# Two layer ends of a float32 encoder trunk: other orders on VectorE and ScalarE, sums of squares on VectorE, one chunk of x on a second queue

## The chip, the cores and the metric

One core of one Trainium2 chip runs the whole kernel. The metric is device time in microseconds of one execution; 0.2% of it, about 2.3 us, is what a measurement of this kernel can tell from no change.

## The reference

The input is x, 512 tokens of 1024 features in float32. Two layers follow, each with an attention part and a dense part, and one last RMSNorm:

```python
for l in range(2):
    h = rmsnorm(x, attn_norm[l])
    proj = h @ w_in[l]                       # 1024 -> 3072: q, k, v of two kinds of heads
    sb_out = stick_breaking_attention(...)   # 8 heads of 64
    df_out = rmsnorm(differential_attention(rope(q), rope(k), v, lam)) * (1 - lambda_init)
    x = x + concat(sb_out, df_out) @ w_o[l]
    h = rmsnorm(x, mlp_norm[l])
    u = square(relu(h @ w_ff1[l]))           # 1024 -> 4096
    x = x + u @ w_ff2[l]                     # 4096 -> 1024
return rmsnorm(x, final_norm)
```

## The kernel before

**Layout.** x lies transposed in SBUF: 8 chunks of 128 features (partitions) by 512 tokens. The host hands over the weights cut into pieces of 128 x 1024.

**Products.** Each float32 operand is split into a rounded part (`hi`, written by ScalarE with a copy, L116 for weights, L228 for activations) and a residue (`lo`, written by VectorE with a subtraction, L117 and L229). A product is three matmuls: hi*hi (L281), hi*lo or lo*hi (L282, L283). So TensorE waits for ScalarE's part in the first and for VectorE's part in another. A scheduler orders each engine's instructions by its own costs; `behind(a, b)` (and `in_order`, which chains it) fixes that `a` stands after `b` on one engine.

**Start.** The 8 chunks of x, and the first two weight pieces in four parts of two chunks each, are loaded by SP's queue in one row (L187, L190); ScalarE's queue loads only the gains (L184). Then chunk by chunk `make_h` (L227) writes `h_hi` and `h_lo`, and `split_part` (L103) splits the weights. DMA completions are kept on eight semaphore lanes, which SP's and ScalarE's loads share in program order, so each load waits for the one eight places ahead of it.

**Middle of a layer.** `wo(0)` (L691) adds the second half of the output projection to x, one chunk (`db`) after another: VectorE adds the PSUM bank to x (L704), `make_h` writes the chunk of the next h, `add_sq` (L233) squares it on ScalarE (L237) and adds the square to `ssq` on GpSimd (L238). In the dense part `rms_a` (L244) transposes and reduces `ssq` on TensorE and VectorE, takes the power -1/2 on GpSimd and writes diagonals; `rms_b` spreads the result. It runs beside the first matmuls of the dense part, since the row scale is applied after the product (L824).

**End of a layer.** w_ff2 is applied by a Strassen-like scheme: seven products (`FORMS`: 11, x3, x2, 22, x1, 21, x4), each 256 x 512 in two banks, which `gather` (L849) adds into SBUF tiles `y`. Tiles are then combined: `merge` (L858) is an accumulating DMA, `join` (L855) a VectorE add over 128 x 1024. After product x1 the join of x1 into x3 and that of x1 into 22 follow; product 21 and product x4 remain. `place(tb, j)` says where a finished block lies: tokens tb (128 each), feature half j; half 1 of tokens 0 and 1 lies in x3, of tokens 2 and 3 in 22; half 0 in x4 and 21. In layer 0, `back(c)` (L873) transposes finished blocks on TensorE and adds them to x; its four first calls stand between the matmuls of products 21 and x4. In layer 1 the last norm is worked out on the finished blocks: `square` (ScalarE, with a sum per row), `root` (a VectorE sum L887 and GpSimd power L889), `weigh` (VectorE times the final gain, L894), and `store`: either ScalarE scales a weighed block (L900) or VectorE scales and weighs at once (L902), then a DMA writes it out (L904), from ScalarE's queue for weighed blocks and from SP's for the others. Two lists, `first` for VectorE and `squares` for ScalarE, hold the order.

Of the kernel before, what the change touches and what calls it, by code (L numbers as in the profile page):

```python
# [85 lines left out]
class _Weights:  # L86
    def __init__(self, nc, dram, rawp, splp):
        self.nc, self.dram, self.rawp = nc, dram, rawp
        self.loaded = self.split = self.used = self.turn = 0
        self.raw, self.tiles, self.home, self.then = {}, {}, {}, {}  # L90
        self.depth = 3
        self.pools = [splp]
        self.owner = {}

    def load(self, n):
        while self.loaded < min(n, len(_RING)):
            i = _RING[self.loaded]
            t = self.rawp.tile([P, 1024], F32, tag="raw", name=f"raw{i}")
            self.nc.sync.dma_start(t, self.dram[self.loaded])
            self.raw[i] = t  # L100
            self.loaded += 1

    def split_part(self, i, a, b):  # L103
        nc = self.nc
        if i not in self.tiles and i in self.home:
            self.tiles[i] = self.home[i]
        if i not in self.tiles:
            k = self.spot(i)
            self.owner[k] = i
            self.turn = k + 1  # L110
            hi = self.pools[k // 2].tile([P, 1024], F32R, tag="whi", name=f"whi{i}")
            lo = self.pools[k // 2].tile([P, 1024], F32R, tag="wlo", name=f"wlo{i}")
            self.tiles[i] = (hi, lo)
        hi, lo = self.tiles[i]
        raw = self.raw[i]
        h = nc.scalar.activation(hi[:, a:b], raw[:, a:b], AF.Copy)  # L116
        self.last = h, nc.vector.tensor_tensor(  # L117
            out=lo[:, a:b], in0=raw[:, a:b], in1=hi[:, a:b].bitcast(F32), op=ALU.subtract)

# [32 lines left out]
def trunk(ctx, tc, xT, w, w2, gains, gfin, lamv, cos, sin, out):  # L152
    nc = tc.nc
# [29 lines left out]
    g_all = cp.tile([P, 42], F32, tag="g", name="g_all")  # L183
    nc.scalar.dma_start(g_all, gains)  # L184
    raws = [wraw.tile([P, 1024], F32, tag="raw", name=f"raw{i}") for i in range(2)]
    for c in range(KC):
        nc.sync.dma_start(x[:, c, :], xT[c])  # L187
        if c % 2 == 0:
            for i in range(2):
                nc.sync.dma_start(raws[i][:, c * P : (c + 2) * P], w[i][:, c * P : (c + 2) * P])  # L190
# [126 lines left out]
    for l in range(L):  # L317
        with ExitStack() as actx:
# [27 lines left out]
            if l == 0:  # L346
                for c in range(KC):
                    if c % 2 == 0:
                        for i in range(2):
                            W.split_part(i, c * P, (c + 2) * P)  # L350
                    opened = make_h(c, gcol("attn", 0, c))
                W.split = 2
            else:
                pts, opened = opened_by.pop()
# [336 lines left out]
            def wo(half):  # L691
                for j in range(4):
                    u = W.next("o")
                    for dd in range(2):
                        db = 2 * j + dd
                        pt = bank("mm" if half else "any", f"wo{l}{half}{db}")
                        for e in range(4):
                            a = u[0][:, e * 256 + dd * P : e * 256 + dd * P + P]
                            b_ = u[1][:, e * 256 + dd * P : e * 256 + dd * P + P]
                            mh, ml = (md_hi, md_lo) if half else (ms_hi, ms_lo)  # L700
                            three(pt, (a, b_), (mh[:, e, :], ml[:, e, :]), e == 0, e == 3)
                            if e < 3:
                                yield 3 * 0.216
                        nc.vector.tensor_add(x[:, db, :], x[:, db, :], pt)  # L704
                        if half == 0:
                            make_h(db, gcol("mlp", l, db))
                            add_sq(db, db == 0, tt)
                        yield 3 * 0.216

            def dense(pts):  # L710
# [58 lines left out]
        with ExitStack() as fctx:  # L769
# [82 lines left out]
                return done  # L852

            def join(to, by):
                nc.vector.tensor_add(y[to], y[to], y[by])  # L855

            def merge(to, by):
                nc.gpsimd.dma_start(  # L858
# [37 lines left out]
            def store(tb, j, weighed):  # L896
                o = place(tb, j)
                r = fin[:, 4 * tb + 7 : 4 * tb + 8]
                if weighed:
                    done = nc.scalar.activation(o, o, AF.Copy, scale=r)  # L900
                else:
                    done = nc.vector.scalar_tensor_tensor(  # L902
                        out=o, in0=o, scalar=r, in1=(cos_t, sin_t)[j], op0=ALU.mult, op1=ALU.mult)
                (nc.scalar if weighed else nc.sync).dma_start(out[tb, :, 512 * j : 512 * j + 512], o)  # L904
                return done

            def in_order(*steps):
# [18 lines left out]
            for g in range(GROUPS):  # L926
# [28 lines left out]
                for f, form in enumerate(FORMS):  # L955
# [6 lines left out]
                    for n, (c, i, r) in enumerate(work):  # L962
                        if c not in held:
                            held[c] = W.next("f")
                        u = held[c]
                        _, hi, lo = forms[2 * c + i]
                        rs = slice(r * P, r * P + P)
                        mine = [m for m, e in enumerate(work) if e[2] == r]
                        three(to[r], (hi[:, SIDE[form], rs], lo[:, SIDE[form], rs]), wpair(u, i, 512),
                              n == mine[0], n == mine[-1])  # L970
                        if tail and last and n == 3:
                            first = [gather("x4", to, (0,))]
                            squares = [square(tb, 0) for tb in (2, 3, 0)]
                            first += [weigh(2, 1), root(2), root(3), weigh(3, 1), root(0)]
                            squares.append(store(2, 1, True))
                        if end and not last and (form, n) in (("21", 5), ("21", 7), ("x4", 1), ("x4", 3)):
                            h = back({"21": 4, "x4": 6}[form] + (n % 4 == 3))
                    if tail:
# [12 lines left out]
                    elif form == "22":  # L991
                        join("22", "x2")
                    elif form == "x1":
                        join("x3", "x1")
                        join("22", "x1")
                        if last:
                            for tb in (0, 1, 2, 3):
                                square(tb, 1)
                            for tb in (0, 1):
                                weigh(tb, 1)  # L1000
            if last:
                first += [gather("x4", to, (1,)), store(0, 0, False), None, store(2, 0, False)]
                squares += [square(1, 0), store(3, 1, True), store(0, 1, True)]
                first[-2] = root(1)
                in_order(*first, store(1, 0, False), store(3, 0, False))
                in_order(*squares, store(1, 1, True))
            else:
                W.pools.pop()
# [76 lines left out]
```

## Time and profile before

| | |
|---|---|
| median of 3 runs | 1161.31 us (1161.12 to 1162.6) |
| profiled execution | 1163.8 us, of it span 1162.0 us |
| granted TensorE clock | 0.998 |
| TensorE matmuls | 1146.6 us busy, 99% of the span |
| VectorE, ScalarE, GpSimd busy | 852.9, 606.2, 191.8 us |
| DMA | 171.67 MB, mean 148 GB/s |

The span is the profiled execution from its first to its last instruction or transfer. "Busy" of TensorE includes overlap of pipelined matmuls, so stalls are read from the starts of consecutive matmuls, which follow each other every 0.227 us where nothing waits. In a timeline row the first number is the start in us, the second the length; an "x2" merges neighbours; the bracket tells how long the engine was idle and who ended it. DVE is VectorE, ACT ScalarE, POOL GpSimd, SPq and ACTq the DMA-issuing side of two engines.

### The profile page before, as it was taken

What the parts mean: (1) busy time and instruction counts of PE and PEld (TensorE: products, weight loads), DVE (VectorE), ACT (ScalarE), POOL (GpSimd) and SP (SyncE); (2) the same over time, 40 slices, a digit from 0 to 9 for tenths busy, and PEclk for the clock granted to TensorE, in tenths of its full rate; (3) what the DMA queues carried; (4) which work ended last, traced back from release to release, by engine and by line L of the source; (5) the groups of instructions that cost most, each with busy time, mean ns of one, the idle gap of its engine ahead of it and who ended that gap; (6) DMA issues with size and microseconds to landing.
All of it is one profiled execution on the core that took longest, in us unless ns stands there. A gap on an engine that the chain in (4) does not pass through costs nothing.

```text
span 1162.0 us, 15297 instructions
## 1 busy us (share of the span) xinstructions
PE 1146.6 (99%) x5458; PEld 951.7 (82%) x5458; DVE 852.9 (73%) x1385; ACT 606.2 (52%) x1075; POOL 191.8 (17%) x271
## 2 busy tenths in 40 slices
PE   9999999999999999999999999999999999999996
PEld 6888888878888888888778888888888888888885
DVE  7888788777556757767888878877676577676676
ACT  6456666545645445445344566665465354453554
POOL 1011543131101001002000125332310010010021
PEclk9999999999999999999999999999999999999999
DMA  7546433146764755737526553432757557467185
GB/s 245 157 145 188 128 109 120 63 177 178 193 178 94 202 158 106 213 134 128 144 73 180 145 165 118 136 91 74 241 121 192 170 92 207 154 99 237 52 155 146
DMA packets 57291, 171.67 MB, mean 148 GB/s; under 512 B 7168, under 2 KB 8192, under 8 KB 57216
## 3 DMA queue, kind: packets, MB, share of 16 engines
q1 hardware_dynamic: 45840, 130.83, 33.9%
q0 software_dynamic: 10656, 38.80, 19.2%
q8 instruction: 43, 0.70, 0.3%
q10 hardware_dynamic: 720, 1.07, 0.2%
q14 instruction: 32, 0.26, 0.1%
HBM read 138.17 MB, written 2.10 MB: 121 GB/s over the span
## 4 chain that ended last, share of the span: by engine, by line
PE 83%; issue 5%; DMA 5%; DVE 4%; ACT 2%; POOL 1%; POOLq 0%; SPq 0%; DVEq 0%; ACTq 0%
PE f L282 9%; PE f L283 9%; PE f L281 9%; PE x L281 4%; PE x L283 4%; PE x L282 4%; PE wo L281 2%; PE wo L282 2%; DMA q<-in_w 2%; PE wo L283 2%; DMA yx<-yx 2%; DVE wlo L117 1%; PE T1s L567 1%; PE T0s L567 1%; DVE h_lo L229 1%
## 5 line engine op out<-in xcount | busy, mean ns | idle before, releaser
L282 PE MATMUL f<-h_lo,whi 128*128 128x512 f32 x512 | 199.3, 389 | 1.0 <-DVE h_lo L229 1.0
L281 PE MATMUL f<-h_hi,whi 128*128 128x512 f32 x512 | 199.7, 390 | 0.0
L116 ACT ACTIVATE whi<-raw 128x1024 fp32r<-128x1024 f32 (+1 forms) x130 | 131.9, 1019 | 129.7 <-PE f L282 40.1
L283 PE MATMUL f<-h_hi,wlo 128*128 128x512 f32 x512 | 199.3, 389 | 0.0
L116 ACT ACTIVATE whi<-q 128x512 fp32r<-128x512 f32 x224 | 128.5, 624 | 120.6 <-PE x L283 45.8
L117 DVE TENSOR_TENSOR wlo<-raw,whi 128x1024 fp32r<-128x1024 f32 (+1 forms) x130 | 153.7, 1187 | 45.1 <-ACT whi L116 44.4
L117 DVE TENSOR_TENSOR wlo<-q,whi 128x512 fp32r<-128x512 f32 x224 | 146.0, 686 | 49.2 <-ACT whi L116 49.0
L282 PEld LDWEIGHTS f<-h_lo,whi 128*128 128x128 f32 x512 | 96.1, 188 | 21.3 <-DVE h_lo L229 1.4
L283 PEld LDWEIGHTS f<-h_hi,wlo 128*128 128x128 f32 x512 | 96.1, 188 | 20.1
L281 PEld LDWEIGHTS f<-h_hi,whi 128*128 128x128 f32 x512 | 96.1, 188 | 19.7
L225 DVE TENSOR_TENSOR Al<-F,Ah 128x256 fp32r<-128x256 f32 (+2 forms) x96 | 74.4, 778 | 44.1 <-ACT Ah L224 44.1
L797 POOL DMA_DIRECT2D q<-in_w x48 | 41.9, 874 | 388.1 <-DVE wlo L117 368.2
L282 PE MATMUL x<-wlo,Ah 128*128 128x512 f32 x256 | 99.7, 390 | 0.7 <-DVE wlo L117 0.7
L281 PE MATMUL x<-whi,Ah 128*128 128x512 f32 x256 | 99.9, 390 | 0.0
L283 PE MATMUL x<-whi,Al 128*128 128x512 f32 x256 | 99.6, 389 | 0.0
L224 ACT ACTIVATE Ah<-F 128x256 fp32r<-128x256 f32 (+2 forms) x96 | 67.2, 703 | 50.4 <-DVE F L833 48.5
L824 DVE SCALAR_TENSOR_TENSOR F<-f,rbc 128x512 f32<-128x512 f32 x64 | 43.5, 687 | 64.9 <-PE f L283 57.6
L825 ACT ACTIVATE F<-F 128x512 f32<-128x512 f32 x64 | 39.7, 624 | 37.2 <-DVE F L824 37.1
L282 PEld LDWEIGHTS x<-wlo,Ah 128*128 128x128 f32 x256 | 48.1, 188 | 11.0 <-DVE wlo L117 1.1
L283 PEld LDWEIGHTS x<-whi,Al 128*128 128x128 f32 x256 | 48.0, 188 | 10.1
L281 PEld LDWEIGHTS x<-whi,Ah 128*128 128x128 f32 x256 | 48.1, 188 | 9.8
L228 ACT ACTIVATE h_hi<-x,g_all 128x512 fp32r<-128x512 f32 x32 | 22.4, 718 | 28.7 <-DVE x L704 17.5
(1055 smaller groups left out, 2556.8 us busy)
## 6 DMA issues: line engine op xcount, KB each, us to landing
raw<-in_w SPq DMA_DIRECT2D x126, 512.0 KB, 4.1
q<-in_w SPq DMA_DIRECT2D x64, 512.0 KB, 4.3
q<-in_w POOLq DMA_DIRECT2D x64, 512.0 KB, 5.4
yx<-yx POOLq DMA_DIRECT2D x6, 512.0 KB, 6.7
x<-in_xT SPq DMA_DIRECT2D x8, 256.0 KB, 4.5
raw<-in_w SPq DMA_DIRECT2D x8, 128.0 KB, 4.4
yx<-y POOLq DMA_DIRECT2D x2, 512.0 KB, 5.7
y<-y POOLq DMA_DIRECT2D x2, 512.0 KB, 8.7
```

What stands on the lines that cost most here:

```text
L116: h = nc.scalar.activation(hi[:, a:b], raw[:, a:b], AF.Copy)
L117: self.last = h, nc.vector.tensor_tensor(out=lo[:, a:b], in0=raw[:, a:b], in1=hi[:, a:b].bitcast(F32), op=ALU.subtract)
L224: nc.scalar.activation(hi, src, AF.Copy)
L225: nc.vector.tensor_tensor(out=lo, in0=src, in1=hi.bitcast(F32), op=ALU.subtract)
L228: a = nc.scalar.activation(h_hi[:, c, :], x[:, c, :], AF.Copy, scale=g)
L281: nc.tensor.matmul(pt, ah, bh, start=first, stop=False)
L282: nc.tensor.matmul(pt, ah, bl, start=False, stop=False)
L283: nc.tensor.matmul(pt, al, bh, start=False, stop=last)
L567: nc.tensor.transpose(pt[:, off : off + P], u["w"][qi][:, kb * P : (kb + 1) * P], ident)
L797: nc.gpsimd.dma_start(t, quad(g, q, c), accum_op=ALU.add)
L824: nc.vector.scalar_tensor_tensor(out=t, in0=pt, scalar=0.0, in1=rbc, op0=ALU.max, op1=ALU.mult)
L825: nc.scalar.activation(t, t, AF.Square)
```

## The change

Five edits, all at the start of layer 0 and at the ends of both layers' parts:

1. Chunk 1 of x is loaded from ScalarE's queue, behind the gains; SP's row has one load less.
2. For the first quarter of the first two weight pieces the rounding, too, is done by VectorE (`eager`).
3. `add_sq` in the middle of both layers adds on VectorE instead of GpSimd (7 adds a layer).
4. After product x1 the join into 22 stands ahead of that into x3, by `in_order`.
5. In the last norm both `weigh` of half 1 of tokens 2 and 3 stand ahead of the first gather of x4 on VectorE, `store(2, 0)` stands ahead of the second gather, `store(3, 1)` ahead of `square(1, 0)` on ScalarE, and `store(3, 0)` ahead of `store(1, 0)`; all stores but the last, (1, 1), are issued by SP.

```diff
+    def round(self, o, src):
+        if self.eager:
+            return self.nc.vector.tensor_copy(o, src)
+        return self.nc.scalar.activation(o, src, AF.Copy)
...
-        h = nc.scalar.activation(hi[:, a:b], raw[:, a:b], AF.Copy)
+        h = self.round(hi[:, a:b], raw[:, a:b])
...
+    nc.scalar.dma_start(x[:, 1, :], xT[1])
     for c in range(KC):
-        nc.sync.dma_start(x[:, c, :], xT[c])
+        if c != 1:
+            nc.sync.dma_start(x[:, c, :], xT[c])
...
                         for i in range(2):
+                            W.eager = c == 0
                             W.split_part(i, c * P, (c + 2) * P)
+                        W.eager = False
...
-                            add_sq(db, db == 0, tt)
+                            add_sq(db, db == 0, tt, nc.vector)
...
-                (nc.scalar if weighed else nc.sync).dma_start(out[tb, :, 512 * j : 512 * j + 512], o)
+                (nc.scalar if (tb, j) == (1, 1) else nc.sync).dma_start(out[tb, :, 512 * j : 512 * j + 512], o)
...
-                            first = [gather("x4", to, (0,))]
+                            first = [weigh(2, 1), weigh(3, 1), gather("x4", to, (0,))]
                             squares = [square(tb, 0) for tb in (2, 3, 0)]
-                            first += [weigh(2, 1), root(2), root(3), weigh(3, 1), root(0)]
+                            first += [root(2), root(3), root(0)]
                             squares.append(store(2, 1, True))
+                            first.append(store(2, 0, False))
+                            squares.append(store(3, 1, True))
...
-                        join("x3", "x1")
-                        join("22", "x1")
+                        in_order(join("22", "x1"), join("x3", "x1"))
...
-                first += [gather("x4", to, (1,)), store(0, 0, False), None, store(2, 0, False)]
-                squares += [square(1, 0), store(3, 1, True), store(0, 1, True)]
-                first[-2] = root(1)
-                in_order(*first, store(1, 0, False), store(3, 0, False))
+                first += [gather("x4", to, (1,)), store(0, 0, False)]
+                squares += [square(1, 0), store(0, 1, True)]
+                first.append(root(1))
+                in_order(*first, store(3, 0, False), store(1, 0, False))
```

As built, the change also moves neighbours: at the start the residues of the second quarter (two L117) stand ahead of chunk 2's `h_lo` on VectorE, no longer behind it, and on ScalarE the second and third `h_hi` follow the first at once; at both joins the second half of a w_ff2 weight residue (L117) now stands right behind the join into x3, in layer 1 ahead of three `weigh`s that it followed; the transposes of the first `rms_a` stand one matmul earlier; and a few roundings, squares and residues of the dense parts' first blocks change places on ScalarE and VectorE.

More of the change, by code (lines that the diff above doesn't have):

```diff
@@ L91, in __init__ @@
         self.depth = 3
+        self.eager = False
         self.pools = [splp]
@@ L854, in join @@
             def join(to, by):
-                nc.vector.tensor_add(y[to], y[to], y[by])
+                return nc.vector.tensor_add(y[to], y[to], y[by])
             def merge(to, by):
```

## The prediction

> **What bounds the kernel now.** I read the page first, then TensorE's waits, then timelines around each wait that the change touches.
>
> ```profile
> span 1162.0 us, 15297 instructions
> PE 1146.6 (99%) x5458; PEld 951.7 (82%) x5458; DVE 852.9 (73%) x1385; ACT 606.2 (52%) x1075; POOL 191.8 (17%) x271
> ```
>
> TensorE is busy for 99% of the span, and the change leaves its matmuls as they are. So it can win only what TensorE waits, and the two ends at which it has nothing to do. Its waits, longest first:
>
> ```profile
> PE f L282 <- DVE h_lo L229: 1.0, 1, 1.0
> PE p L281 <- ACT h_hi L228: 0.8, 1, 0.8
> PE S1d L477 <- DMA st1d3q<-hl1d3k: 0.7, 1, 0.7
> PE x L282 <- DVE wlo L117: 0.7, 1, 0.7
> PE yT L876 <- DVE y L855: 0.7, 1, 0.7
> ```
>
> Four of these five lie where the change works: f at the middle of layer 0, p at the start, x at the end of layer 1, yT at the end of layer 0. S1d lies in layer 1's attention, which it leaves alone. Between these places TensorE's starts follow each other without a hole and every load is triggered by work on the engines, so I take time won at one place as kept to the end.
>
> **Middle of layer 0 (adds of squares): 1.18 us won.**
>
> ```profile
> 249.74 1.38 POOL L238 TENSOR_TENSOR ssq<-ssq,sq 128x512 f32<-128x512 f32 x1 [0.84 <-ACT sq L237]
> ...
> 249.90 1.76 DVE L229 SCALAR_TENSOR_TENSOR h_lo<-x,g_all,h_hi 128x512 fp32r<-128x512 f32 x1
> ...
> 250.08 0.39 PE L283 MATMUL f<-h_hi,wlo 128*128 128x512 f32 x1
> 250.31 0.39 PE L281 MATMUL f<-h_hi,whi 128*128 128x512 f32 x1
> 251.72 0.50 PE L282 MATMUL f<-h_lo,whi 128*128 128x512 f32 x1 [1.02 <-DVE h_lo L229]
> ...
> 818.28 0.69 DVE L704 TENSOR_TENSOR x<-x,wo 128x512 f32<-128x512 f32 x1
> 819.76 0.75 DVE L229 SCALAR_TENSOR_TENSOR h_lo<-x,g_all,h_hi 128x512 fp32r<-128x512 f32 x1 [0.79 <-ACT h_hi L228]
> 821.00 0.69 DVE L704 TENSOR_TENSOR x<-x,wo 128x512 f32<-128x512 f32 x1 [0.49 <-PE wo L283]
> 821.91 1.23 DVE L117 TENSOR_TENSOR wlo<-raw,whi 128x1024 fp32r<-128x1024 f32 x1 [0.23 <-ACT whi L116]
> 823.06 0.75 DVE L229 SCALAR_TENSOR_TENSOR h_lo<-x,g_all,h_hi 128x512 fp32r<-128x512 f32 x1
> 823.15 1.79 POOL L238 TENSOR_TENSOR ssq<-ssq,sq 128x512 f32<-128x512 f32 x1 [1.47 <-ACT sq L237]
> 825.78 0.39 PE L282 MATMUL f<-h_lo,whi 128*128 128x512 f32 x1
> ...
> 14.91 0.69 DVE L238 TENSOR_TENSOR ssq<-ssq,sq 128x512 f32<-128x512 f32 x1 [0.29 <-ACT sq L237]
> ```
>
> The seventh `h_lo` of layer 0 runs beside a GpSimd add and takes 1.76 us; the same one in layer 1 started first, takes 0.75, and there GpSimd's add is long (1.79). TensorE lost 251.72 - 250.31 - 0.23 = 1.18 us to this; layer 1 lost nothing.
>
> The add on VectorE costs 0.69 (last row, the same operation in the start). For a pair of chunks VectorE then needs, by the layer 1 rows less 0.09 overlap each: x 0.60, wait for `h_hi` 0.88, `h_lo` 0.66, add 0.60, x 0.60, wlo 1.14, `h_lo` 0.66, add 0.60 = 5.74 us. TensorE's pair is 24 matmuls of 0.227 = 5.44. VectorE falls behind by 0.3 a pair on top of the first add's 0.6: about 1.2 at the last pair, whose x then comes at 819.5 instead of 818.28 and whose last `h_lo` ends 5.2 later, at 824.7. Its matmul is due at 825.78: 1.0 us spare in layer 1, and as much in layer 0, where the matmul is due at 250.53. So the wait goes. Queued behind the adds are the next weight residues, needed a block (5.4 us) later, and the transposes of `ssq`, which stand after the first block. Six adds stand ahead of the last `h_lo`, so 0.17 more for each would use that up; beyond it each further 0.17 costs 1.0 us a layer. Bounds: 0.9 to 1.2.
>
> **End of layer 0 (order of the joins): 0.85 us won.**
>
> ```profile
> 566.53 1.23 DVE L855 TENSOR_TENSOR yx<-yx,yx 128x1024 f32<-128x1024 f32 x1 [1.14 <-DMA yx<-yx]
> 567.67 1.22 DVE L855 TENSOR_TENSOR y<-y,yx 128x1024 f32<-128x1024 f32 x1
> ...
> 567.86 0.41 PE L876 MATMUL yT<-edge,yx 128*128 128x128 f32 x2 [0.28 <-issue]
> 568.95 0.44 PE L876 MATMUL yT<-edge,y 128*128 128x128 f32 x2 [0.68 <-DVE y L855]
> ```
>
> VectorE idles 1.14 us for the accumulating DMA into x3, then does both joins. The join into 22 waits for no DMA and takes 1.22: put first, it fits into that hole but for 0.1. The x3 join stays where it is, and the two x transposes still start at 567.86. The two y transposes follow 0.24 later instead of 1.09: 0.85. What is late next is that DMA, so the 0.4 lost ahead of 567.86 remains. Bounds 0.6 (the hole filled less well) to 1.25 (both waits gone).
>
> **End of layer 1: 0.95 us won.**
>
> ```profile
> 1148.77 0.68 DVE L117 TENSOR_TENSOR wlo<-q,whi 128x512 fp32r<-128x512 f32 x1
> 1149.37 0.68 DVE L849 TENSOR_TENSOR y<-y,21130_10400 128x512 f32<-128x512 f32 x1
> ...
> 1153.02 0.69 DVE L849 TENSOR_TENSOR yx<-yx,x 128x512 f32<-128x512 f32 x1 [0.20 <-PE x L283]
> ...
> 1149.51 0.50 PE L282 MATMUL x<-wlo,Ah 128*128 128x512 f32 x1 [0.71 <-DVE wlo L117]
> ...
> 1152.06 2.12 POOL L889 TENSOR_TENSOR fin<-fin,mhalf 128x1 f32<-128x1 f32 x3 [10.18 <-DVE fin L887]
> ...
> 1153.16 0.72 ACT L900 ACTIVATE y<-y,fin 128x512 f32<-128x512 f32 x1 [1.07 <-POOL fin L889]
> ...
> 1157.81 0.33 SPq L904 DMA_DIRECT2D out_xT<-y  x1
> ...
> GB/s 0 0 0 0 0 0 225 440 379 266 0 82 430 379 389 287 440 369 430 379 440 369 420 399 410 400 420 399 389 430 389 430 379 440 277 0 0 0 0 0
> ```
>
> The last row is the DMA rate from 1153.5 to 1161.5 in slices of 0.2: after one hole (at 1155.5) the eight stores of 0.256 MB stream at about 390 GB/s, 0.67 us each, until 1160.5. So the end is the first store's time plus eight transfers plus holes, not the last block's arithmetic.
>
> TensorE: the residue that x waits for (1148.77) stood behind both joins and two `weigh`s. As in layer 0, the join into 22 now fills VectorE's wait for the DMA, and the `weigh`s follow the residue: it comes a join (1.14) and two steps of 0.60 sooner, and the waiting of 0.7 goes. But VectorE's row, not TensorE, sets the rest. Ahead of the gathers of 21 (1149.37) it has one join less and one `weigh` more, so they come 0.55 earlier (1.14 - 0.60); the second `weigh` then stands ahead of the first gather of x4, which stays where it was. With the gathers of 21 come the squares and roots of tokens 2 and 3 and the first power; ScalarE's first store moves from 1153.16 to about 1152.6. The stores of (2,0) and (3,1) are ready at 1153.4 and 1153.9 instead of after the second gather, so the hole of 0.35 closes: 0.55 + 0.35 = 0.9, and 0.05 for ScalarE, which no longer issues three stores in its row. The added wait: the second gather of x4 is queued behind `store(2, 0)`, which waits for GpSimd's power, and comes at 1153.3 instead of 1153.02 though its matmuls end 0.9 sooner. The last blocks (1,0) and (1,1) are then issued at about 1156.9, when the stream has work until 1158.2; that is their cover, 0.5 us after the transfer's start-up. SP issues seven stores of 0.33 each and is never the last. Bounds: 0.35 (the power comes no earlier, only the hole closes) to 1.4.
>
> **Start: 0.3 us won, the least certain.**
>
> ```profile
> 2.12 4.73 DMA x<-in_xT
> ...
> 2.00:4.00 2.00, 2.00 (x6) 0.71 (x5) 0.21 (x2) 0.88 (x3) 0.29 (x4) 1.00 0.97 265
> 4.00:5.00 1.00, 1.00 (x6) 0.37 (x4) 0.46 (x1) 0.81 (x2) 0.00 (x0) 1.00 0.67 70
> ...
> 5.08 0.42 ACT L116 ACTIVATE whi<-raw 128x256 fp32r<-128x256 f32 x1 [0.27 <-DMA raw<-in_w]
> ...
> 6.87 1.34 ACT L228 ACTIVATE h_hi<-x,g_all 128x512 fp32r<-128x512 f32 x2 [1.38 <-DMA x<-in_xT]
> 8.11 0.71 ACT L116 ACTIVATE whi<-raw 128x256 fp32r<-128x256 f32 x2
> ...
> 8.96 0.75 DVE L117 TENSOR_TENSOR wlo<-raw,whi 128x256 fp32r<-128x256 f32 x2
> ...
> 9.70 0.39 PE L282 MATMUL p<-h_lo,whi 128*128 128x512 f32 x1
> ```
>
> Chunk 1 is issued at 2.12 and lands at 6.85; `h_hi` of chunks 1 and 2 follow. From the second queue it goes out behind the gains alone, not behind three loads. Meanwhile the second weight piece, landed at 5.08, bounds from below: on VectorE a rounding (0.2 to 0.4, the wlo row's half at most), `h_lo`, wlo, `h_lo` of chunk 1 = 2.2, so 7.3, and the 14th matmul (9.70 before, `h_lo` of chunk 2) at 8.7: 1.0 won at most. From the other side: `h_lo` of chunk 2 now stands behind two residues. If chunk 2 lands no sooner (its `h_hi` starting at 7.54), `h_hi` 0.70, two roundings 0.71, the second residue 0.50 and `h_lo` 0.75 put that matmul at 10.2: 0.5 lost. If it lands in chunk 1's old place, 6.87: 0.1 won. In the fifth microsecond (the two rows that begin with a stretch; their last three columns are clock, DMA share and GB/s) the DMA share is 0.67 at 70 GB/s, room for part of chunk 1 earlier, so I take 0.3. On VectorE the two added roundings lie in its idle time ahead of chunk 1; without that they would cost 0.2 to 0.4 each.
>
> The Trainium skill (DMA: Bandwidth & Descriptors, "Rules for kernel authors") says that spreading DMAs over several issuing engines gives no bandwidth, since all use the same 16 engines, and saves issue time alone. By that rule the gain would be at most one issue slot of SP, 0.45, and the sum 3.4; no run so far shows two such queues under load at the start.
>
> **Sum.** 1.18 + 0.85 + 0.95 + 0.3 = 3.3 us. The profiled execution took 1163.8 (span 1162.0 and 1.8 around it), so 1160.5 with a profile; the median without is 1161.31, so 1158.0.
>
> **Rivals.**
> - The two queues share the DMA engines, and chunk 1 pushes the first weight pieces back; start -0.5. Total 2.5, 1158.8. For it: the share is 0.97 already from 2 to 4. Against it: 0.67 right after. Chance 0.12.
> - The end of layer 1 stays bound by VectorE and the power: only 0.35 there. Total 2.7, 1158.6. Chance 0.10.
> - One middle or end edit does not do what it says (VectorE is late for another reason and TensorE waits as before) beside one of these: total 1.3 to 2.0, about 1159.6. Chance 0.15.
> - Slower: the adds make VectorE the bound of both middles. TensorE begins to wait when an add takes a step of 0.77 (0.60 + 0.17), and the whole is slower from 1.04 on. At GpSimd's 1.38 each of six adds costs 0.78 more, 4.7, less the 1.0 spare 3.7 in each layer; layer 0 had 1.18 of it before. With 2.1 won at the other places: 1161.31 + 3.7 + 2.5 - 2.1 = 1165.4. Against it: the row of 0.69. Chance 0.05.
> - My forecast, 1158.0: 0.58.
>
> The range reaches from all upper bounds together (1.2 + 1.25 + 1.4 + 1.0 = 4.85, 1156.5) to a gain of 1.0 (1160.3), which takes in all but the slower case. Faster by over 0.2% (2.3 us): 0.77, from the forecast and nearly all of the first two rivals; same 0.17; slower 0.06.
>
> **What would show it.** In the changed profile: f <- `h_lo` and yT <- y gone from TensorE's waits, or yT down to 0.1; every `h_lo` near 0.75; x <- wlo gone; the first store near 0.55 earlier against the last matmuls' old place and no zero in the DMA row; 14th matmul of p before 9.7. Wrong: a new wait on `h_lo` in either middle, a new wait at the transposes of `ssq`, or `h_hi` waiting for x beyond 6.9.

## The result

The changed kernel took 1158.43 us (median of 10 runs, 1157.34 to 1161.88) against 1161.78 for the kernel before beside it (10 runs, 1160.39 to 1163.42). The ratio is 0.9976, 95% interval 0.9967 to 0.9984: 2.8 us won, between 1.9 and 3.8. A second comparison, under after_again below, gave 0.9968 (0.9959 to 0.9978), 3.7 us. The forecast was 1158.0, from 1161.31, and 3.3 won.

The profiled execution took 1157.94 us. Its page begins:

```profile
span 1155.8 us, 15280 instructions
...
PE 1145.5 (99%) x5458; PEld 952.6 (82%) x5458; DVE 856.4 (74%) x1401; ACT 606.6 (52%) x1073; POOL 171.0 (15%) x257
```

TensorE's waits in it, all that the view lists (total us, times, longest):

```profile
PE warm L214 <- POOL edge L208: 1.4, 1, 1.4
PE S1d L487 <- DMA st1d3q<-hl1d3k: 0.6, 1, 0.6
PE yT L886 <- issue: 0.4, 1, 0.4
```

The waits for `h_lo`, `wlo`, `y` and `h_hi` are gone. The two profiled spans differ by 6.2 us, nearly twice what the medians differ by (3.35). Where that comes from is the larger part of what follows: the starts of the same matmul in both traces show it to a tenth of a microsecond, and so do the traces of the experiments, each of which has some stages with the code of before and some with the code after.

The middle of layer 0, timeline of the changed kernel (start, us, engine, line, operation, tiles; in brackets the idle time before and its releaser):

```profile
242.05 0.75 DVE L237 SCALAR_TENSOR_TENSOR h_lo<-x,g_all,h_hi 128x512 fp32r<-128x512 f32 x1
...
243.31 0.68 DVE L714 TENSOR_TENSOR x<-x,wo 128x512 f32<-128x512 f32 x1
...
244.78 0.75 DVE L237 SCALAR_TENSOR_TENSOR h_lo<-x,g_all,h_hi 128x512 fp32r<-128x512 f32 x1 [0.79 <-ACT h_hi L236]
...
245.45 0.68 DVE L246 TENSOR_TENSOR ssq<-ssq,sq 128x512 f32<-128x512 f32 x1
...
246.05 0.68 DVE L714 TENSOR_TENSOR x<-x,wo 128x512 f32<-128x512 f32 x1
...
246.65 1.22 DVE L123 TENSOR_TENSOR wlo<-raw,whi 128x1024 fp32r<-128x1024 f32 x1
...
247.79 0.75 DVE L237 SCALAR_TENSOR_TENSOR h_lo<-x,g_all,h_hi 128x512 fp32r<-128x512 f32 x1
...
248.45 0.68 DVE L246 TENSOR_TENSOR ssq<-ssq,sq 128x512 f32<-128x512 f32 x1
...
249.61 0.39 PE L290 MATMUL f<-h_lo,whi 128*128 128x512 f32 x1
```

Every `h_lo` takes 0.75 (the last took 1.76), the adds 0.68, and the matmul that waited 1.02 starts without a wait, 1.07 after its `h_lo` is done (248.54). The forecast's row for a pair of chunks is there: from the sixth `h_lo` to the eighth it takes 5.74, as forecast.

The end of layer 0, timeline:

```profile
563.27 1.22 DVE L865 TENSOR_TENSOR y<-y,yx 128x1024 f32<-128x1024 f32 x1
564.40 1.22 DVE L865 TENSOR_TENSOR yx<-yx,yx 128x1024 f32<-128x1024 f32 x1
...
565.73 0.41 PE L886 MATMUL yT<-edge,yx 128*128 128x128 f32 x2 [0.36 <-issue]
565.97 0.38 PE L886 MATMUL yT<-edge,y 128*128 128x128 f32 x2
```

The two kinds of transposes are 0.24 apart, where they were 1.09. VectorE no longer waits for the accumulating DMA; the joins stand back to back. Counted by the start of the same matmul, this end is 0.84 shorter.

The end of layer 1: the joins, the first gather of 21, the roots, the powers and ScalarE's first two stores:

```profile
1139.43 1.22 DVE L865 TENSOR_TENSOR y<-y,yx 128x1024 f32<-128x1024 f32 x1
1140.57 1.22 DVE L865 TENSOR_TENSOR yx<-yx,yx 128x1024 f32<-128x1024 f32 x1
...
1144.12 0.68 DVE L859 TENSOR_TENSOR y<-y,21130_10400 128x512 f32<-128x512 f32 x1
...
1146.51 0.33 DVE L897 TENSOR_SCALAR fin<-fin 128x1 f32<-128x1 f32 x2
...
1146.81 1.85 POOL L899 TENSOR_TENSOR fin<-fin,mhalf 128x1 f32<-128x1 f32 x3 [9.21 <-DVE fin L897]
...
1147.41 1.34 ACT L910 ACTIVATE y<-y,fin 128x512 f32<-128x512 f32 x2
```

The DMA rate from 1147.5 to 1155.5 in slices of 0.2 us:

```profile
GB/s 0 0 0 0 0 0 0 184 379 430 379 420 399 399 410 410 410 379 440 379 420 389 430 389 430 389 420 379 440 379 440 379 430 154 0 0 0 0 0 0
```

Once it has begun, the stream of stores has no hole. From the start of the last matmul to the end of the span it was 9.42, and is 8.26.

The start, chunks 1 and 2 of `x` as `h_hi` takes them up, and below them the fifth microsecond (last three columns: clock, DMA share, GB/s):

```profile
4.70 0.72 ACT L236 ACTIVATE h_hi<-x,g_all 128x512 fp32r<-128x512 f32 x1 [0.24 <-DMA x<-in_xT]
5.86 0.72 ACT L236 ACTIVATE h_hi<-x,g_all 128x512 fp32r<-128x512 f32 x1 [0.43 <-DMA x<-in_xT]
```

```profile
4.00:5.00 1.00, 1.00 (x4) 0.35 (x3) 0.69 (x2) 0.76 (x2) 0.00 (x0) 1.00 1.03 357
```

Before, chunk 1 was taken up at 6.87 and chunk 2 right behind it; the microsecond that moved 70 GB/s moves 357.

### The profile page after: what moved, and what is told of

The parts are those of the page before. It is cut to its first block, busy times and chain, and to the rows that moved or that the text cites. A ratio compares the mean times of both kernels' runs of the same rounds, so it can differ in the third digit from the quotient of the medians.

```text
span 1155.8 us, 15280 instructions
## 1 busy us (share of the span) xinstructions
PE 1145.5 (99%) x5458; PEld 952.6 (82%) x5458; DVE 856.4 (74%) x1401; ACT 606.6 (52%) x1073; POOL 171.0 (15%) x257
## 4 chain that ended last, share of the span: by engine, by line
PE 93%; DVE 3%; DMA 2%; ACT 1%; issue 1%; POOL 0%; POOLq 0%; ACTq 0%; DVEq 0%
PE f L290 10%; PE f L289 10%; PE f L291 10%; PE x L290 4%; PE x L289 4%; PE x L291 4%; PE wo L289 3%; PE wo L291 3%; PE wo L290 3%; DMA q<-in_w 1%; DVE wlo L123 1%; PE T1s L577 1%; PE T0s L577 1%; PE p L289 1%; PE p L290 1%
```

## Experiments: each part alone

Four kernels are the one before with one part of the change; they share 33 runs of before (median 1163.11).

```diff
# start_alone: chunk 1 on ScalarE's queue, first two roundings on VectorE
+    nc.scalar.dma_start(x[:, 1, :], xT[1])
...
+        h = self.round(hi[:, a:b], raw[:, a:b])
# adds_alone
+                            add_sq(db, db == 0, tt, nc.vector)
# joins_alone, in layer 0 only
+                            in_order(join("22", "x1"), join("x3", "x1"))
# tail_alone: in_order of the joins in layer 1, weighs, gathers, stores, SyncE's queue
```

> Only the two edits of the start: chunk 1 of x on ScalarE's queue, and the first two roundings on VectorE. The two traces so far show the 14th matmul of p at 9.70 before and near 8.86 after, 0.8 to 0.9 sooner, where the prediction had 0.3. Theory (the hole in the fifth microsecond is filled by the second queue, and the rest of the program carries the gain to the end): starts of the same matmul 0.9 sooner from p on to the last block, time 0.9 us less than before. Rival (the prediction's price; the rest was the draw of that one trace): 0.3 us sooner. Second rival: 0.9 is won at p and lost again at a later wait, time 0 to 0.3 less.

> Only the adds of squares in the middles moved to VectorE, in both layers. Theory: layer 0 loses its wait of f for h_lo, 1.18 to 1.3 us sooner from there on, layer 1 stays without a wait, time 1.2 less than before. Rival (VectorE bound in the middle): a new wait of f or wo for h_lo in one layer, gain under 0.5 or a loss.

> Only the order of the two joins at the end of layer 0. Theory: the wait of yT for y of 0.7 and the 1.09 between the two kinds of transposes shrink, 0.85 us sooner from there on, time 0.85 less. Rival (the DMA that accumulates into x3 is late in its turn): 0 to 0.3. In this trace the attention of layer 1, which no edit touches, shows whether its waits (tv1w 0.6, S1d 0.7 before; the first gone after the change) go with the code or with the run.

> Only the edits at the end of layer 1: order of the joins, weighs, gathers and stores, and the stores on SyncE's queue. Theory A (as predicted): 0.95 us less, the wait of x for wlo gone and the stores 0.9 sooner. Theory B (by the pair of traces: the wait gone, 0.99, and 1.16 more behind the last matmul): 2.1 less. They differ in the distance from the last matmul's start to the end of the span: A 9.4 as before, B 8.3.

| part | median us | ratio (95%) | mean span less than before's | mean time outside the span |
|---|---|---|---|---|
| start | 1162.61 | 1.0001 (0.9991 to 1.0011) | 0.52 | 2.14 |
| adds | 1161.56 | 0.9992 (0.9984 to 1.0001) | 1.41 | 1.76 |
| joins | 1163.18 | 1.0002 (0.9993 to 1.0011) | 0.28 | 2.13 |
| tail | 1161.76 | 0.9992 (0.9983 to 1.0001) | 1.82 | 2.15 |

No part alone is told from no change by its time; each interval is 2 us wide. So the times alone decide between few of the theories: of the first ones, only that of joins_alone lies outside its interval, by little (at most 0.8 won), and so does theory B of tail_alone (at most 2.0 won). The spans add up to 4.0 us. Three of the four also have 0.35 us more outside the span than before (1.78), where the whole change has 0.2 to 0.3 more (2.0 to 2.05); nothing recorded lies there, and what it is stays open. With it taken three times the parts give 3.0 us, with the whole change's share taken once 3.8.

The traces say more. **start_alone** has no loss in the middle of layer 0, though its adds are on GpSimd as before, but the same loss in layer 1. Its rows, layer 0 and then layer 1:

```profile
230.80 0.75 DVE L237 SCALAR_TENSOR_TENSOR h_lo<-x,g_all,h_hi 128x512 fp32r<-128x512 f32 x1
...
230.84 1.86 POOL L246 TENSOR_TENSOR ssq<-ssq,sq 128x512 f32<-128x512 f32 x1 [16.81 <-ACT sq L245]
...
805.24 1.87 DVE L237 SCALAR_TENSOR_TENSOR h_lo<-x,g_all,h_hi 128x512 fp32r<-128x512 f32 x1
...
805.27 1.29 POOL L246 TENSOR_TENSOR ssq<-ssq,sq 128x512 f32<-128x512 f32 x1 [16.80 <-ACT sq L245]
```

GpSimd's first add and VectorE's second `h_lo` of the middle start within 0.04 us of each other, and one of them then takes longer than alone: the `h_lo` 1.87 for 0.75, or the add 1.86 for 1.29. Where VectorE loses, it is late and loses again in each later pair, and TensorE waits 1.0 at the end; where GpSimd loses, nobody waits. Over the six traces with plain adds on GpSimd, VectorE lost in 5 of 12 middles: in layer 0 in four of four with the old start and in none of two with chunk 1 on ScalarE's queue, in layer 1 in one of six. So the term of 1.18 is right where it is lost, which in layer 0 was every traced middle behind the old start. Behind the new start, without any other edit, layer 0 lost nothing, so the forecast's terms for start and middle can't simply be added; why the start should matter for what happens at 231 us isn't shown. The Trainium skill (SBUF — State Buffer, "Summary: rules for kernel authors") says that where a VectorE instruction with two SBUF inputs meets a GpSimd one that reads SBUF, the second to issue is blocked until the first is done. The lengths agree (1.86 and 1.87 are nearly 1.29 and 0.75 together). Which of the two loses can't be read from the recorded starts: `h_lo` is recorded first, by 0.03 to 0.04, in all 12 middles and is the one that is late in 5.

**joins_alone** wins little, because the hole that the join of 22 was to fill isn't 1.14 in every run. Its rows, and under them the one row of tail_alone, which has the old order there; then ScalarE's rounding of a weight piece some 6 us ahead of the joins, in before and in joins_alone:

```profile
565.86 1.22 DVE L855 TENSOR_TENSOR y<-y,yx 128x1024 f32<-128x1024 f32 x1
566.99 1.22 DVE L855 TENSOR_TENSOR yx<-yx,yx 128x1024 f32<-128x1024 f32 x1
...
568.31 0.41 PE L876 MATMUL yT<-edge,yx 128*128 128x128 f32 x2 [1.00 <-issue]
568.56 0.38 PE L876 MATMUL yT<-edge,y 128*128 128x128 f32 x2
```

```profile
566.74 1.23 DVE L855 TENSOR_TENSOR yx<-yx,yx 128x1024 f32<-128x1024 f32 x1 [0.57 <-DMA yx<-yx]
```

```profile
559.30 1.15 ACT L116 ACTIVATE whi<-q 128x512 fp32r<-128x512 f32 x2 [2.77 <-DMA q<-in_w]
```

```profile
559.84 2.19 ACT L116 ACTIVATE whi<-q 128x512 fp32r<-128x512 f32 x4 [2.62 <-DMA q<-in_w]
```

In the seven traces with the old order VectorE waited 1.13 to 1.15 for the DMA into x3 in four, 0.84, 0.83 and 0.57 in the others. Where the hole is short, VectorE comes late: that rounding, which waits for its load, starts between 8.20 and 9.21 after the 2600th matmul, and in all fourteen traces VectorE is free for the joins 6.0 to 6.1 behind it, while the DMA lets the x3 join go at 15.4 to 15.9. So what varies here is the landing of a weight load that no edit touches. The join of 22 takes 1.13 in front of x3, so that x3 comes up to 0.56 later than it could, and in joins_alone TensorE waits 1.00 ahead of the x transposes. From the 2600th to the 2690th matmul, seven traces with the old order take 0.25 us more than before's on the mean, six with the new one and the same matmul order 0.42 less: 0.7 won, between 0.3 and 1.1 by the draw.

**tail_alone** has no wait of x for `wlo`, and 8.79 behind the last matmul, halfway between theory A (9.4) and theory B (8.3). Its 1.82 in the span is nearer B (2.1) than A (0.95), but its time, 0.1 lost to 2.0 won, takes in A and not B. What this end is worth is worked out below from the rows.

## Experiments: middle and attention

```diff
# adds_fenced: before, and GpSimd's add waits for h_lo of its chunk
+                            h = make_h(db, gcol("mlp", l, db))
+                            s = add_sq(db, db == 0, tt)
+                            if db:
+                                tc.add_manual_dep(s[1].ins, h[1].ins.name, mybir.DependencyInfo(
+                                    mybir.DependencyClass.Sync, mybir.DependencyReason.DATA), reason="order")
# adds_twice: the changed kernel, a second instruction of the add's size
+                                nc.vector.tensor_tensor(out=ssq, in0=ssq, in1=ssq, op=ALU.max)
```

> The kernel before, with the adds of squares still on GpSimd, but each made to wait until h_lo of its chunk is done, so that the two never run side by side. In four traces with the adds on GpSimd, GpSimd's add and VectorE's second h_lo start 0.03 us apart in each middle; in 4 of 8 middles VectorE's takes 1.87 (and three later ones 1.77), in the other 4 GpSimd's takes 1.86. Theory (a shared access that one of two nearly simultaneous instructions wins, and the loser's lateness repeats it in each pair; the adds' place is only a way to avoid the overlap): no h_lo over 0.75 in either layer, no wait of f for h_lo, time as with the adds on VectorE, 1.2 to 1.5 less than before on the mean of runs. Rival (the adds on VectorE won because of the order on VectorE or ScalarE): f still waits 1.0 in one layer, time as before.

> The changed kernel with a second instruction of the add's size behind each add of squares in both middles (a maximum of ssq with itself, which leaves it as it is). By the prediction's model VectorE has 1.0 us spare at the last h_lo; six more steps of 0.60 ahead of it cost 3.6 - 1.0 = 2.6 us in each layer, 5.2 in all, seen as waits of f or wo for VectorE. Rival (more slack than the model had, since steps of VectorE moved ahead of TensorE's needs or the transposes wait instead): under 1.5 a layer.

adds_fenced took 1161.75 us (11 runs), ratio 0.9996 (0.9986 to 1.0007). In its trace no `h_lo` takes over 0.76, no add over 1.30, and f doesn't wait in either layer; the two middles are as short as with the adds on VectorE. So the overlap of the two instructions is the cause of the loss, and the add's place only a way around it: that part of the theory is shown. That it is worth 1.2 us on the mean of runs is not: the mean span is 0.55 less than before's (1161.04, 18 runs), two of the 11 runs lie over 2 us above the others, and the interval takes in both theories.

adds_twice took 1160.06 in its one run; its waits of TensorE are

```profile
PE warm L214 <- POOL edge L208: 1.4, 1, 1.4
PE yT L888 <- issue: 1.2, 1, 1.2
PE S1d L487 <- issue: 0.6, 2, 0.4
```

and none is in a middle. The forecast's model gave 2.6 us a layer; the sections cost nothing in layer 0 and 0.1 in layer 1. The model had added VectorE's wait for `h_hi` (0.79 in the row at 244.78 above) to its work, as if it were a load; a further instruction lies in that wait. Between the second and the last `h_lo` of layer 0 the changed kernel has three such waits, 2.38 in all, and 1.07 behind the last. With five instructions more ahead of the last `h_lo`, adds_twice has 0.20 of idle time left there, and 0.41 from the end of that `h_lo` (249.51) to its matmul (249.92). So the spare was about 3.4 a layer and not 1.0, and adds_twice uses most of it. Also the planner moved the sums' transposes three matmuls back and put the sixth of the second instructions behind the last `h_lo`. The slower rival counted only the 1.0 against its 4.7 a layer, and was priced too high by the other 2.4.

The attention of layer 1, which no edit touches, was 0.95 us shorter in the trace of after than in before's. ScalarE's rows of before there, then of the changed kernel's second trace:

```profile
661.87 0.63 ACT L937 ACTIVATE cos_t<-cos_t 128x512 f32<-128x512 f32 x1 [2.83 <-DMA cos_t<-in_gfin]
663.33 0.63 ACT L938 ACTIVATE sin_t<-sin_t 128x512 f32<-128x512 f32 x1 [0.83 <-DMA sin_t<-in_gfin]
663.87 0.61 ACT L224 ACTIVATE hl1d3k<-u1d3q 128x512 fp32r<-128x512 f32 x1
```

```profile
659.43 0.63 ACT L948 ACTIVATE sin_t<-sin_t 128x512 f32<-128x512 f32 x1
659.97 0.62 ACT L232 ACTIVATE hl1d3k<-u1d3q 128x512 fp32r<-128x512 f32 x1
```

The final gains are loaded and scaled some 480 us before they are used, and `hl1d3k`, on which the next scores depend, stands behind the scalings in ScalarE's row. In the 12 traces with this code the section takes 19.92 to 20.53 us in the eight in which ScalarE waits at most 0.44 for `sin_t`, and 21.02 to 21.39 in the four in which it waits 0.81 to 1.00.

```diff
# late_scale: the changed kernel, both scalings behind the last copy of layer 1's x forms
+                    behind(nc.scalar.activation(cos_t, cos_t, AF.Copy, scale=math.sqrt(D)), moved[0])
+                    behind(nc.scalar.activation(sin_t, sin_t, AF.Copy, scale=-math.sqrt(D)), moved[0])
```

> The changed kernel, and the two scalings of the final gains (cos_t, sin_t on ScalarE, in the middle of layer 1's attention) moved back to the MLP of layer 1. In the five traces so far ScalarE waits there for the DMA of sin_t between 0 and 1.00 us, hl1d3k stands behind it in ScalarE's row, and the section from the 3100th to the 3200th matmul takes from 1.5 us more (start_alone) to none more (tail_alone), with the same code there in all. Theory (the landing of that DMA, not any edit, makes this section vary): the section comes out at the shortest of those, or shorter by up to 0.3, vT1w doesn't wait; on the mean of runs 0.3 to 0.6 less than the changed kernel, a gain over before of 3.2 to 3.8 in place of 2.8 to 3.3, and a narrower spread. Rival (another cause): the section varies as before and the time is that of the changed kernel.

```profile
659.53 0.63 ACT L232 ACTIVATE hl1d3k<-u1d3q 128x512 fp32r<-128x512 f32 x1 [3.19 <-DVE u1d3q L463]
```

`hl1d3k` now waits for its own input alone, and S1d and vT1w wait no longer. The section is 1.79 shorter than before's, 0.57 below the shortest of the twelve, more than the 0.3 forecast, and 1.2 below their mean; in late_both below, with the same edit, it is 0.30 below the shortest. The whole: 1158.69 us (8 runs), 0.9970 (0.9959 to 0.9981), 3.5 us won, between the two results of the changed kernel, and the runs lie no closer together (3.5 us from lowest to highest). That those DMAs, by ScalarE's row, make the section vary is shown; its worth in the time isn't.

## Experiments: start and end

```diff
# own_queue: the changed kernel, chunk 1 second on SyncE's own queue
-    nc.scalar.dma_start(x[:, 1, :], xT[1])
+        if c == 0:
+            nc.sync.dma_start(x[:, 1, :], xT[1])
# queue_alone: before, with this line and the loop without chunk 1, roundings on ScalarE
+    nc.scalar.dma_start(x[:, 1, :], xT[1])
```

> The changed kernel with chunk 1 of x on SyncE's own queue, issued second, right behind chunk 0, in place of ScalarE's queue. Four traces of before's start have the 60th matmul 0.2 us around a mean, two of the changed start 0.26 and 0.62 sooner than that mean. Theory (issue time alone: what counts is that chunk 1 goes out ahead of the weight pieces): chunk 1 lands within 0.2 of the changed kernel's and the 60th matmul as in the changed kernel. Rival (a second queue brings bandwidth while the first is under load): chunk 1 or the first weight pieces land 0.4 to 0.8 later and the 60th matmul falls back to before's.

> The kernel before with chunk 1 of x on ScalarE's queue and nothing else; the first two roundings stay on ScalarE. In five traces with chunk 1 on SyncE's queue the DMA rate falls to 57 to 92 GB/s from 4 to 5 us; in four with it on ScalarE's queue it is 355 to 375, and the 200th matmul comes 0.57 sooner on the mean (47.03 to 47.58 against 47.80 to 48.11). Theory (the queue is what brings the gain): no hole from 4 to 5 us, the 200th matmul at 47.2 to 47.6. Rival (the roundings bring it, since ScalarE is in the way): the hole is gone and the 200th matmul is at 47.8 to 48.1.

The stretch with the lowest rate in joins_alone (old start), own_queue and queue_alone:

```profile
4.00:5.00 1.00, 1.00 (x6) 0.44 (x4) 0.50 (x1) 0.78 (x2) 0.00 (x0) 1.00 0.64 82
```

```profile
6.00:7.00 1.00, 0.80 (x4) 0.51 (x3) 0.96 (x4) 0.00 (x0) 0.00 (x0) 1.00 0.61 185
```

```profile
4.00:5.00 1.00, 1.00 (x4) 0.35 (x3) 0.46 (x2) 0.82 (x2) 0.00 (x0) 1.00 0.93 316
```

With chunk 1 second on SyncE's queue it lands at 4.13, sooner than in the changed kernel (4.68), its `h_hi` follows the first at once, from 3.71, and the 60th matmul starts at 17.57, in the range of two queues with the roundings (17.25 to 17.79) and ahead of before's start (17.77 to 18.08). So far issue time alone would do. But the hole comes two microseconds later, chunk 2 is taken up at 7.36, the stretch from the 80th to the 130th matmul takes 11.82 (11.45 to 11.67 with one queue, 11.23 to 11.49 with two), and the 200th matmul starts at 47.98, as before (47.80 to 48.11 in six traces, mean 47.92); the run took 1160.52. With the second queue alone there is no hole from 4 to 5 us and the 200th matmul starts at 47.00 (the run took 1161.38); with the roundings too at 47.03 to 47.58 (six traces, mean 47.36; start_alone 47.44, between its two theories). So two queues win 0.56 us at the 200th matmul, and the one trace without the roundings has all of it; whether they bring anything of their own can't be told from one trace. Between 2 and 7 us 1.21 to 1.28 MB arrive with one queue in six traces, 1.51 to 1.66 with two in seven, 1.43 in own_queue.

The rule of the Trainium skill that the forecast weighed (DMA: Bandwidth & Descriptors, "Rules for kernel authors") doesn't cover these five microseconds: more data arrive with two queues, and before's hole isn't for want of issued loads, since four, issued from 2.12 to 3.54, are under way in it and land from 6.85 on. That issuing earlier on one queue doesn't give the gain rests on the one trace of own_queue and on the 200th matmul alone. Why one queue leaves the hole isn't shown.

```diff
# end_joins: before, with the order of the joins changed in layer 1 only
+                            in_order(join("22", "x1"), join("x3", "x1"))
```

> The kernel before with the order of the two joins changed at the end of layer 1 alone; weighs, gathers, roots and stores as the planner puts them then, the stores on the queues of before. With all the edits of that end TensorE's wait of x for wlo is gone in five traces of five (1.08 won on the mean of before's) and the time behind the last matmul is 0.2 to 1.2 less, 0.65 on the mean. Theory (the joins bring the first part, the order of weighs and stores the second): the wait is gone, the part behind the last matmul is 9.4 as before, time 1.1 less than before. Rival (the part behind the last matmul comes from the joins too): 8.8 there, time 1.7 less.

```profile
1144.22 1.22 DVE L855 TENSOR_TENSOR y<-y,yx 128x1024 f32<-128x1024 f32 x1
1145.75 1.23 DVE L855 TENSOR_TENSOR yx<-yx,yx 128x1024 f32<-128x1024 f32 x1 [0.32 <-DMA yx<-yx]
...
1148.38 0.68 DVE L849 TENSOR_TENSOR y<-y,21130_10400 128x512 f32<-128x512 f32 x1
...
1151.62 0.68 DVE L894 TENSOR_TENSOR y<-y,sin_t 128x512 f32<-128x512 f32 x1
...
1151.67 2.12 POOL L889 TENSOR_TENSOR fin<-fin,mhalf 128x1 f32<-128x1 f32 x3 [9.27 <-DVE fin L887]
...
1152.77 0.72 ACT L900 ACTIVATE y<-y,fin 128x512 f32<-128x512 f32 x1 [1.08 <-POOL fin L889]
```

It took 1163.47 us (12 runs), ratio 1.0000 (0.9986 to 1.0013), an interval that takes in the theory's 1.1; so the trace has to tell. TensorE's wait is gone, and from the 5300th matmul the last one comes 1.05 sooner than on the mean of the six old-order traces, but 9.90 follow it instead of 9.42: neither theory had that. The gather of 21 comes 2.63 after the join of x3 instead of 4.08. The weighs then stand between the gathers, so the first power comes 3.29 behind the gather instead of 2.69, and 5.92 behind the x3 join instead of 6.77. From that power to the end it is 9.95 in both. So the end follows the power, on VectorE's row, and not the last matmul: it comes 0.86 sooner from the x3 join, and 0.58 from the 5300th matmul, since the x3 join itself was 0.29 late in this trace.

With those rows the end can be accounted for. Times are from the start of the x3 join; old order in six traces, new in seven, each the same within 0.04:

| step | old order | new order |
|---|---|---|
| x3 join to the first gather of 21 | 4.08 | 3.54 |
| that gather to the first power | 2.69 | 2.69 |
| power to ScalarE's first store | 1.10 | 0.60 |
| first store's DMA issue to the end | 8.10 | 7.69 |

That is 1.45, and the x3 join itself starts 0.27 sooner on the mean of the traces (the DMA that it waited for varies here too): 1.7. The joins' order alone gives 0.86 of the 1.45, as end_joins shows; the rest, 0.59, comes with the order of weighs and stores. The 0.50 in the third line goes with what VectorE does beside the first power: in the old order, as in end_joins' row of 1151.62, a `weigh` of 0.68, in the new one (changed kernel, from 1146.84 to 1147.38) nothing. GpSimd's first power is then 0.57 long instead of 1.07. No run changes this alone, so as a cause it is argued.

## Experiment: a faster version

```diff
# late_both: late_scale, and the transposes of y at the end of layer 0 one step later
+            LATER = (("21", 6), ("x4", 0), ("x4", 2), ("x4", 4))
+                        if end and not last and (form, n) in LATER:
+                            h = back(4 + LATER.index((form, n)))
# after_again: the changed kernel once more, beside it
```

> The changed kernel with two more edits: the late scaling of the final gains as in late_scale, and at the end of layer 0 each of the four steps that transpose y back is put one step (three matmuls, 0.68 us) later between the matmuls of 21 and x4. In all traces with the new join order TensorE waits ahead of the first of these transposes, 0.4 to 1.2 us, since two joins of 1.13 stand back to back on VectorE. Theory: 0.68 us of other matmuls cover most of that, the section from the 2600th to the 2690th matmul shortens by 0.35 to 0.68, and with the late scaling the whole is 0.9 to 1.4 less than the changed kernel run beside it. Rival: the later steps come too late for the next layer's first matmuls and a wait of p for h_lo takes back what was won: equal to late_scale, 0.4 to 0.8 less than the changed kernel.

> The changed kernel once more, beside the others. Sections of its other traces give: start 0.57 less than before, middles 1.3 less in one layer out of two, end of layer 0 0.4 to 0.8 less, end of layer 1 with its tail 1.7 less: 4.0 to 4.4 less in the span. Theory (these sections carry the whole): 3.3 to 4.2 less than before in the time. Rival (the first comparison stands): 2.8 less.

late_both: 1158.07 us (7 runs), 0.9964 (0.9949 to 0.9978), 4.2 us won. after_again: 1159.39 (12 runs), 0.9968 (0.9959 to 0.9978), 3.7 us, inside its forecast from the sections, 3.3 to 4.2; its interval (2.6 to 4.8) takes in the rival's 2.8 too. The section at the end of layer 0 is 0.6 to 0.8 shorter than in the changed kernel's two traces, without a wait at the transposes; 0.3 of it is lost again by the 3100th matmul. The lead of late_both over the changed kernel is 1.3 by medians and 0.7 by means; the two intervals overlap so far that it isn't shown to be one.

Its trace, which is of its slowest run, also shows a loss of 2.5 us in layer 0's MLP, where no code differs; own_queue lost 0.35 there, the others at most 0.04:

```profile
297.74 1.15 ACT L107 ACTIVATE whi<-q 128x512 fp32r<-128x512 f32 x2 [3.06 <-DMA q<-in_w]
...
300.57 0.50 PE L289 MATMUL x<-whi,Ah 128*128 128x512 f32 x1 [1.35 <-ACT Ah L232]
```

A rounding of weights, first in ScalarE's row, waited 3.06 for a load on GpSimd's queue, and what stood behind it came late. The wait itself is hardly longer than in the trace of after (2.60), but counted from the 1350th matmul the rounding starts 3.0 later, and GpSimd issued this load and the two before it 2.5 later. Why it fell behind isn't shown. Most kernels have a few runs 2 to 3 us above their others; whether this is their cause wasn't seen, since they have no trace.

## Why the prediction was right, and where not

- **Sum: right, in part by luck.** 3.3 forecast, 2.8 (1.9 to 3.8) and 3.7 (2.6 to 4.8) measured. The sections add up to more, about 4.2 (1.29, 0.7, 1.7 and 0.56), since the end of layer 1 was priced 0.8 too low; 0.2 to 0.3 of it goes outside the span.
- **Middle, 1.18:** the mechanism and the amount are right where it occurs (1.29 in the pair of traces, by start of the same matmul): adds_fenced, which only keeps the add and the `h_lo` apart, is as fast in the middles. What was wrong is to take one profile's loss as fixed to layer 0: it was lost in 5 of 12 middles, in layer 0 with the old start each time, once in layer 1, and in layer 0 never with the new start. The 1.0 us spare was there (1.07), but "beyond it each further 0.17 costs 1.0 us a layer" was wrong: 2.4 more lay in the waits for `h_hi`, and twice the adds cost 0.1 in all.
- **End of layer 0, 0.85:** 0.84 in the pair, 0.7 over the traces, 0.46 in joins_alone. The term took the hole of 1.14 as fixed; it is shorter where a weight load lands late, and at 0.57 the join ahead of x3 costs x3 half of its length. The remaining wait was forecast for the DMA's sake; it is there (0.4 to 1.2), but VectorE starts the x3 join right behind the other in six of seven traces, so it is the join in front, and the time at which VectorE comes to it, that sets it.
- **End of layer 1, 0.95:** mis-sized, 1.7, beyond its upper bound of 1.4. The first 0.55 is there within 0.01 (4.08 to 3.54), as is the closing of the hole (0.41 for 0.40). Missing were 0.50 between power and store, and 0.27 for the wait that varies. That VectorE's row and not TensorE sets the end is shown by end_joins.
- **Start, 0.3:** 0.56 over the traces, 1.08 in the pair, at the 200th matmul; its bounds were 0.5 lost to 1.0 won. Where the forecast had left open whether chunk 2 lands sooner, it does: it is taken up at 5.86, and before behind chunk 1, at 7.54. One trace with the queue alone has the whole gain, so the roundings aren't needed for it.
- **Base:** the profile of before was a slow draw: 0.95 of the 6.2 between the two spans lies in the attention's `sin_t`, and the traces with before's code in a stage are on the mean 0.2 shorter at the start than its own (and 0.25 longer at the end of layer 0). TensorE's wait of 0.6 at `vT1w`, just below those that the forecast lists, belongs to the same stretch and is gone where `sin_t` comes in time. That is why the term at one place has to be read from several traces.

## What to carry to other kernels

A stall read from one profile may be one of two outcomes of a near tie: look whether the same code shows it elsewhere in the same trace (here layer 1 didn't), and price the edit by how often it is lost. In an engine's row count work and waits apart: an added instruction lies in a wait first. Where two engines work towards the end of a stage, find the row that the end follows: in end_joins the last matmul came 1.05 sooner and the end 0.58, as much as the first power did.

## What was not expected of the hardware

- A VectorE `h_lo` (0.75 alone) and a GpSimd add (1.29 alone) that start within 0.04 us: one takes 1.86 to 1.87, and which one differs between traces of the same code (layer 1: one of six).
- From the start of GpSimd's first small power to ScalarE's store that uses it, 0.60 with VectorE idle beside it (seven traces), 1.10 beside a VectorE product of 0.68 (seven traces). In the first case ScalarE itself was busy up to 0.06 before the store, so 0.60 is no more than an upper bound for the power.
- One queue at the start left the fifth microsecond at 57 to 92 GB/s in six traces; with one of its transfers on a second queue it was 316 to 375 in seven.
- The time outside the span is 1.76 to 1.82 in some of these kernels and 2.0 to 2.15 in others, without a recorded reason.
